# Gate and modulation vectors transposed on TensorE and written to DRAM as 512-byte rows

## Chip, core and metric

The kernel runs on one core of a Trainium2 chip. The time is device time in microseconds (us) from start to end of the program. The engines are PE (TensorE; PEld is its weight load), DVE (VectorE), ACT (ScalarE), POOL (GpSimd) and SP (SyncE, which issues all DMAs that matter here; its queue is called SPq in the rows). SP works its DMAs off in order: one that waits for data holds those behind it.

## The reference, cut to what matters

Two trunk layers run on 256 latent tokens `x` and 256 context tokens, of width 1024. Layer 0 is a gMLP mixer and a dense SwiGLU; layer 1 is an RG-LRU mixer and a mixture of 8 experts. Each sub-layer has this frame:

```python
sh1, sc1, gt1, sh2, sc2, gt2 = split(silu(c) @ ada_w[i] + ada_b[i], 6)   # 1024 numbers each
h = rmsnorm(x, norm_g[i, 0]) * (1 + sc1) + sh1
x = x + gt1 * rmsnorm(mixer(h), norm_g[i, 1])
x = x + gt2 * rmsnorm(channel_mixer(rmsnorm(x, norm_g[i, 2]) * (1 + sc2) + sh2), norm_g[i, 3])
```

The context has its own six vectors from `c_ctx`. The gate `gt * norm_g` is one number per channel, the same for all tokens. The last sub-layer also needs scale and shift as rows, since its tokens lie on partitions.

## The kernel before, in words

**Stages.** The weights come as 69 blocks of 1 MB (`in_wA`) in the order of `_weight_order` (L53): gMLP (`v`, `u`, `w`), dense feed-forward (`fg`, `fu`, `fd`), RG-LRU (`lx`, `lg`, `lw`). Each block is split by ACT (L249, the high part `wh`) and DVE (L250, the remainder `wl`), and used in three matmuls per product (L504 to L506 and L520 to L522). After about 880 us the experts run on raw weights (`in_wM`, 336 blocks).

**Stream.** Class `Stream` (L192) issues the loads on SP into a ring of raw buffers, four of them in the stretch at issue. A buffer is loaded again when DVE has read it. Three pairs of `wh`/`wl` buffers hold split weights ahead of PE.

**The adaLN matrix.** From block 3 on, 40 blocks of 1 MB of `in_adaT` stand among the weight blocks in the same ring. DVE multiplies each with the broadcast SiLU vector and sums along the row (L388, tile `dj`), so the six vectors of a layer come out as columns: channel `k*128 + p` lies on partition `p`, column `k`, of a `[128, 8]` tile.

**Columns to rows.** `gate_col` (L434) makes a gate column with two DVE operations (L436, L437). `rows_out` (L440) writes each column to DRAM by one DMA, L443:

```python
nc.sync.dma_start(d[i].rearrange("(k p) -> p k", p=P), c)
```

On the DRAM side neighbours of one partition lie 128 elements apart, so 1024 numbers go out one by one. `rows_in` (L446) reads the row back, broadcast to 128 partitions. There are four places, eight columns in all:

- `grd` (L723): layer 0's first gate for context and latent, written after unit W2 in the code, read into `gr`, used in `finish` (L678) of the first `turn` (L669).
- `gr2d` (L843): layer 0's second gate, after the fourth down-projection unit (`fd` 3), read into `gr2` at once, used in the second `turn`.
- `mrd` (L1005): layer 1's first gate and the coefficients `mca`, `mcb`, read into `mrow` at L1038.
- `god` (L1006): layer 1's second gate, read into `grow` at L1466, for the last step.

**Order.** Every engine runs its own instruction list in order. The lists are not the order of the code: when the program is built, a planner gives each engine the next instruction that is ready by its cost figures, the earlier in the code first. So operations with early data can stand far ahead of their place in the code. PSUM has eight banks, handed out by `bank()` (L275).

Of the kernel before, what the change touches and what calls it, by code (L numbers as in the profile page):

```python
# [9 lines left out]
F32 = mybir.dt.float32  # L10
# [7 lines left out]
P = 128  # L18
D = 1024
# [249 lines left out]
def block_kernel(ctx, tc, xin, pos, cst, rows, wsT, adaS, adaT, wA, lruG, wr, wM, out):  # L269
    nc = tc.nc  # L270
    ACT, DVE, PE = nc.scalar, nc.vector, nc.tensor
# [3 lines left out]
    bank = lambda: psx[0].tile([P, 512], F32, tag="ps", name="ps")  # L275
# [6 lines left out]
    pre = PRE.enter_context(pool("pre"))  # L282

    k = pre.tile([P, NCOL], F32, name="k")
# [6 lines left out]
    ident = perm.tile([P, P], F32, name="ident")  # L291
# [27 lines left out]
    PAIRS = (0, 1)  # L319
    VEC = (1, 0)  # L320
# [110 lines left out]
            do(b0, b1)  # L431
        return a, b, do

    def gate_col(l, s, gi, vv):  # L434
        g = pre.tile([P, 8], F32, name=f"cg{l}{s}{vv}")
        DVE.tensor_add(g, adaC[l, s][:, :, vv], K(f"adab{l}")[:, s * 8:s * 8 + 8])  # L436
        DVE.tensor_mul(g, g, ng(l, gi))  # L437
        return g

    def rows_out(cols, name):  # L440
        d = tc.dram_tile([len(cols), D], F32, name=name)
        for i, c in enumerate(cols):
            nc.sync.dma_start(d[i].rearrange("(k p) -> p k", p=P), c)  # L443
        return d

    def rows_in(dst, d):  # L446
        nc.sync.dma_start(dst, d.partition_broadcast(P))
# [68 lines left out]
    def ws(o, w, cb, c0, c1):  # L516
        wh, wl = w
        for kk in range(8):
            r = slice(kk * 256 + cb * P, kk * 256 + (cb + 1) * P)
            PE.matmul(o, wh[:, r], hThi[:, kk, c0:c1], start=(kk == 0), stop=False)  # L520
            PE.matmul(o, wh[:, r], hTlo[:, kk, c0:c1], start=False, stop=False)  # L521
            PE.matmul(o, wl[:, r], hThi[:, kk, c0:c1], start=False, stop=(kk == 7))  # L522
# [72 lines left out]
    def v_norm():  # L595
        for t in range(4):
            DVE.bn_aggr(mv[:, t], bst[:, t])
        DVE.tensor_scalar(vv_, mv[:, :, 1], EPS, None, op0=ALU.add)
        rsqrt(vr, vv_, 4)
        for t in range(4):  # L600
            DVE.tensor_scalar(v[t], v[t], mv[:, t, 0:1], vr[:, t:t + 1], op0=ALU.subtract, op1=ALU.mult)
# [14 lines left out]
    def u_mm(i):  # L616
        w = st.get()
        bs = [bank(), bank()]
        for cb in range(2):
            ws(bs[cb], w, cb, 0, 512)  # L620
        return bs

    def unit_u(i, bs):
        gu = []
        for cb in range(2):
            g = tmp.tile([P, 512], F32, tag="gu", name="gu")
            ACT.activation(g, bs[cb], AF.Gelu_apprx_tanh)
            gu.append(g)
        for cb in range(2):
            c = 2 * i + cb  # L630
            m = bank()
            for n in range(4):
                PE.matmul(m[:, n * P:(n + 1) * P], v[n][:, c * P:(c + 1) * P], wst[:, i], start=True, stop=True)
            t = tmp.tile([P, 512], F32, tag="t512", name="t")
            DVE.scalar_tensor_tensor(t.rearrange("p (n t) -> p n t", n=4), m.rearrange("p (n t) -> p n t", n=4), gv[:, c:c + 1],
                                     bsr[:, i][:, None, :].to_broadcast([P, 4, P]), op0=ALU.mult, op1=ALU.add)
            DVE.tensor_mul(t, t, gu[cb])
            split(c, t)

    def w_half(q, hf, first):  # L640
        w = st.get()
        banks = [bank() for _ in range(4)]
        ts(banks, pH, pL, w, range(4), 4, True, True, kb0=4 * q)
        for t in range(4):
            ys = ysum[:, t, hf * 512:(hf + 1) * 512]
            if first:
                ACT.copy(ys, banks[t])
            else:
                DVE.tensor_add(ys, ys, banks[t])

    def unit_w(q, first):
        for hf in range(2):
            w_half(q, hf, first)
        for c in range(4 * q, 4 * q + 4):
            prods.pop(c)
# [13 lines left out]
    def turn(last_w, last_mm, first_w, first_mm, X, gr, cf, before_t, nw):  # L669
# [42 lines left out]
                first_mm(n, ws_[n], p)  # L712
        return mid

    bu = [u_mm(0), u_mm(1)]
    v_norm()
    for s in ("U0", "U1", "U2", "W0", "U3", "U4", "W1", "U5", "U6", "W2"):
        if s[0] == "U":
            i = int(s[1])
            unit_u(i, bu[i] if i < len(bu) else u_mm(i))  # L720
        else:
            unit_w(int(s[1]), s == "W0")
    grd = rows_out([gate_col(0, 2, 1, VEC[p]) for p in PAIRS], "grd")  # L723
    w7 = st.get()
    p7 = [[php.tile([P, 512], F32R, tag=n, name=n) for n in ("ph", "pl")] for _ in range(2)]

# [72 lines left out]
    def unit_f(j, evac):  # L799
        w = st.get()  # L800
        banks = []
        for cb in range(2):
            b = bank()
            ws(b, w, cb, 0, 512)
            banks.append(b)
        evac(j, banks)
# [28 lines left out]
    for it in ORDER[24 + 4:]:  # L835
        if it[0] == "fg":
            unit_f(it[1], fg_evac)
        elif it[0] == "fu":
            unit_f(it[1], fu_evac)
        elif it[0] == "fd" and it[2] == 0 and it[1] < 4:  # L840
            unit_w(it[1], it[1] == 0)
            if it[1] == 3:
                gr2d = rows_out([gate_col(0, 5, 3, VEC[p]) for p in PAIRS], "gr2d")  # L843
                gr2 = xcp.tile([P, 2, D], F32, tag="gr", name="gr2")
                rows_in(gr2, gr2d)
    cfl = [coef(1, 0, 1, 0, VEC[p]) for p in PAIRS]
# [32 lines left out]
    def conv(c, b, seg):  # L879
        if c not in xq:  # L880
            xq[c] = php.tile([P, 2, 256], F32, tag="ph" if c < 6 else "pl", name="xq")
        for s in seg:
            src = b[:, 256 * s:256 * s + 256]
            o = xq[c][:, s]
            DVE.tensor_scalar(o, src, cw[:, 16 + c:17 + c], cbias[:, c:c + 1], op0=ALU.mult, op1=ALU.add)
            for kk, off in ((0, -2), (1, -1), (3, 1)):
                lo, hi = max(0, -off), 256 - max(0, off)
                DVE.scalar_tensor_tensor(o[:, lo:hi], src[:, lo + off:hi + off], cw[:, kk * 8 + c:kk * 8 + c + 1], o[:, lo:hi], op0=ALU.mult, op1=ALU.add)
# [21 lines left out]
    def queued():  # L910
        return tc.issue_after(act_last[0].ins) if act_last[0] is not None else nullcontext()
# [25 lines left out]
    def gates_exp(j):  # L937
        R_, I_, T_ = RIT.pop(j)
        hs[j] = php.tile([P, 2, 256], F32, tag="pl", name="hs")
        last = None  # L940
        with queued():
            act_last[0] = ACT.preload_act_table_set("natural_log_exp_and_others")
        with queued():
            for cb in range(2):
                t, i, a = T_[cb], I_[cb], R_[cb]
                ACT.activation(t, t, AF.Ln, bias=tiny[:, 0:1])
                ACT.activation(t, t, AF.Exp, scale=0.5)
                for d in range(2):
                    col = slice(d * 8 + 2 * j + cb, d * 8 + 2 * j + cb + 1)
                    last = ACT.activation(a[:, d], a[:, d], AF.Exp, scale=nspl[:, col])  # L950
                DVE.scalar_tensor_tensor(t, a, 1.0, t, op0=ALU.add, op1=ALU.mult)
                DVE.tensor_tensor(out=i, in0=i, in1=t, op=ALU.mult)
                DVE.tensor_tensor_scan(t[:, 0], a[:, 0], i[:, 0], 0.0, ALU.mult, ALU.add)
                rv = lambda z, s: z[:, 1, 256 * s:256 * s + 256][:, ::-1]
                DVE.tensor_tensor_scan(rv(t, 0), rv(a, 0), rv(i, 0), 0.0, ALU.mult, ALU.add)
                DVE.tensor_tensor_scan(rv(t, 1), rv(a, 1), rv(i, 1), t[:, 1, 0:1], ALU.mult, ALU.add)
                DVE.tensor_add(hs[j][:, cb], t[:, 0, 256:512], t[:, 1, 256:512])
        act_last[0] = last

    def unit_x(j):  # L960
        w = st.get()
        for cb in range(2):
            b = bank()
            ws(b, w, cb, 0, 512)
            conv(2 * j + cb, b, (0, 1))
# [3 lines left out]
    def unit_g(j):  # L969
        w = st.get()  # L970
        b = bank()
        for cb in range(2):
            ws(b[:, cb * 256:(cb + 1) * 256], w, cb, 256, 512)
        gbs[j] = b
# [27 lines left out]
        DVE.tensor_tensor(out=f(yl), in0=h2, in1=f(yh).bitcast(F32), op=ALU.subtract)  # L1002

    mca, mcb, _ = coef(1, 3, 4, 2, 0)
    mrd = rows_out([gate_col(1, 2, 1, 0), mca, mcb], "mrd")  # L1005
    god = rows_out([gate_col(1, 5, 3, 0)], "god")  # L1006
    unit_x(3)
    gates_exp(1)
    unit_g(0)
    gates_sig(2)  # L1010
# [24 lines left out]
    R = ExitStack()  # L1035
    rp = R.enter_context(pool("rp", 1, "right"))
    mrow = hTp.tile([P, 4, D], F32, tag="hThi", name="mrow")
    rows_in(mrow[:, 0:3], mrd)  # L1038
    iot = rp.tile([P, 256], I32, name="iot")
    nc.gpsimd.iota(iot, pattern=[[1, 256]], base=1, channel_multiplier=0)  # L1040
    slot = mp.tile([P, 256], F32, name="slot")
# [421 lines left out]
                DVE.tensor_scalar(Ys[E.s][:, 512:1024], E.base.y[1], E.base.ps, None, op0=ALU.mult)  # L1463
    ACT.preload_act_table_set("sqrt_and_others")
    grow = mw.tile([P, D], F32, name="grow")
    rows_in(grow[:, None, :], god)  # L1466
    mj = ta_.bitcast(BF16)
    ssf = small.tile([P, 4], F32, tag="ss", name="ssf")
    rsf = small.tile([P, 4], F32, tag="rstd", name="rsf")
# [32 lines left out]
```

## Time and profile before

| What | us |
|---|---|
| Median of 3 runs | 1881.88 (1878.27 to 1882.68) |
| The profiled execution | 1881.16 |
| Its span, first to last instruction | 1879.2 |
| PE busy | 1685.1 (90%) |
| DVE busy | 832.9 (44%) |
| ACT busy | 572.3 (30%) |
| Mean granted PE clock | 0.961 of full speed |

Busy time is a mean over stages with different limits. The windows view gives it by stretch: busy time of each engine, instructions in brackets, the granted clock, the busy share of the 16 DMA engines and what they moved. In the timeline each row is an instruction; a square bracket gives how long its engine stood idle before it and what released it.

### The profile page before, as it was taken

The page shows a single profiled execution, that of the slowest core. Times are in us where ns is not written, and L with a number is a line of the kernel's source. Part 1 is how long each engine was busy: PE and PEld are TensorE (multiplying, and loading weights), DVE is VectorE, ACT ScalarE, POOL GpSimd, SP SyncE. Part 2 cuts the span into 40 slices and gives each one's busy share as a digit, 9 for nine tenths or more (in the row PEclk, how much of TensorE's full clock was granted, in tenths as well). Part 3 has the DMA queues.
Part 4 walks back from the last instruction along what each step waited for, and adds up shares of the span by engine and source line. Part 5 has one row for each costly group of instructions (what it writes and reads, how often), then busy time and mean ns, then how long its engine had stood idle before and what let it go on. Part 6 is the DMA issues. An engine that isn't in the chain of part 4 may idle for free. (4 is left out here: it accounts for less than half of the span.)

```text
span 1879.2 us, 21723 instructions
## 1 busy us (share of the span) xinstructions
PE 1685.1 (90%) x8189; PEld 1034.8 (55%) x8189; DVE 832.9 (44%) x1340; ACT 572.3 (30%) x837; POOL 19.4 (1%) x22
## 2 busy tenths in 40 slices
PE   5999999998997999997678789988998999889987
PEld 2888888987885788775324233333433344333332
DVE  3768746566964538896322222224111112222233
ACT  5523224732221227893221112211111112122221
POOL 0000001000000000001000000000000000000000
PEclk8999999999998899999789899999998999999999
DMA  8554424247775622246697769896899899979990
GB/s 355 210 171 157 157 90 158 105 174 175 275 189 182 187 97 79 68 174 270 275 416 308 303 266 379 364 397 262 363 417 419 367 395 360 403 312 388 401 401 23
DMA packets 78629, 492.97 MB, mean 262 GB/s; under 512 B 16240, under 2 KB 16368, under 8 KB 20080
## 3 DMA queue, kind: packets, MB, share of 16 engines
q1 hardware_dynamic: 78448, 490.45, 68.1%
q8 instruction: 127, 2.08, 0.4%
q14 instruction: 54, 0.44, 0.1%
HBM read 489.34 MB, written 1.08 MB: 261 GB/s over the span
## 5 line engine op out<-in xcount | busy, mean ns | idle before, releaser
L1263 PE MATMUL ps<-raw,x 128*64 128x512 f32 (+2 forms) x1792 | 441.7, 613 | 28.3 <-PEq L1351 11.9
L1263 PEld LDWEIGHTS ps<-raw,x 128*64 128x64 f32 (+2 forms) x1792 | 162.8, 143 | 261.5 <-issue 244.7
L1290 PE MATMUL ps<-raw,hx 128*32 128x512 f32 (+2 forms) x1120 | 259.2, 626 | 18.2 <-ACT hx L1282 15.1
L520 PE MATMUL ps<-hThi,wh 128*128 128x512 f32 (+1 forms) x736 | 254.3, 347 | 3.0 <-ACT hThi L373 3.0
L521 PE MATMUL ps<-hTlo,wh 128*128 128x512 f32 (+1 forms) x736 | 253.1, 344 | 1.3 <-DVE hTlo L374 1.3
L522 PE MATMUL ps<-hThi,wl 128*128 128x512 f32 (+1 forms) x736 | 253.5, 345 | 0.0
L1270 DVE TENSOR_TENSOR ta__6625<-ps,ta__6625 64x512 f32<-64x512 f32 x112 | 76.5, 683 | 350.3 <-ACT ta__6625 L1269 350.3
L388 DVE SCALAR_TENSOR_TENSOR dj<-raw,srow 128x1024 bf16<-128x1024 f32 x128 | 156.3, 1221 | 93.3 <-DMA raw<-in_adaT_dram 89.9
L249 ACT CAST wh<-raw 128x2048 fp32r<-128x2048 f32 x69 | 131.4, 1908 | 203.7 <-PE ps L506 95.5
L250 DVE TENSOR_TENSOR wl<-raw,wh 128x2048 fp32r<-128x2048 f32 x69 | 158.8, 2304 | 58.7 <-ACT wh L249 58.2
L1290 PEld LDWEIGHTS ps<-raw,hx 128*32 128x32 f32 (+2 forms) x1120 | 92.3, 138 | 161.9 <-issue 123.1
L1269 ACT COPY ta__6625<-ps 64x512 f32<-64x512 f32 x112 | 65.2, 582 | 302.4 <-PE ps L1263 292.3
L520 PEld LDWEIGHTS ps<-hThi,wh 128*128 128x128 f32 x736 | 138.7, 189 | 21.8 <-ACT hThi L373 3.7
L521 PEld LDWEIGHTS ps<-hTlo,wh 128*128 128x128 f32 x736 | 138.8, 189 | 20.5 <-DVE hTlo L374 1.7
L522 PEld LDWEIGHTS ps<-hThi,wl 128*128 128x128 f32 x736 | 138.9, 189 | 17.5 <-issue 0.5
L504 PE MATMUL ps<-wh,ph 128*128 128x512 f32 x304 | 122.7, 404 | 17.3 <-ACT ph L609 17.3
L506 PE MATMUL ps<-wh,pl 128*128 128x512 f32 x304 | 121.4, 400 | 6.7 <-DVE pl L610 6.3
L1296 DVE TENSOR_TENSOR hx<-hx,ps 128x512 f32<-128x512 f32 x14 | 9.6, 688 | 252.3 <-PE ps L1263 177.8
L505 PE MATMUL ps<-wl,ph 128*128 128x512 f32 x304 | 120.2, 395 | 0.0
L1282 ACT COPY hx<-ps 128x128 f32<-128x128 f32 (+2 forms) x70 | 25.3, 361 | 225.0 <-PE ps L1281 223.3
L1263 PE MATMUL ps<-raw,xu 128*32 128x512 f32 x448 | 69.5, 633 | 21.6 <-DVE accy L1318 11.4
L504 PEld LDWEIGHTS ps<-wh,ph 128*128 128x128 f32 x304 | 58.3, 192 | 30.2 <-ACT ph L609 18.2
(318 smaller groups left out, 1669.2 us busy)
## 6 DMA issues: line engine op xcount, KB each, us to landing
raw<-in_wM_dram SPq DMA_DIRECT2D x336, 1024.0 KB, 13.7
raw<-in_wA_dram SPq DMA_DIRECT2D x69, 1024.0 KB, 4.9
raw<-in_adaT_dram SPq DMA_DIRECT2D x40, 1024.0 KB, 5.4
va<-in_adaS_dram SPq DMA_DIRECT2D x4, 1024.0 KB, 10.6
ysum<-in_xin_dram SPq DMA_DIRECT2D x4, 512.0 KB, 5.3
vb<-in_adaS_dram SPq DMA_DIRECT2D x2, 1024.0 KB, 10.8
srow<-in_adaS_dram SPq DMA_DIRECT2D x2, 1024.0 KB, 12.2
lw<-in_lruG_dram SPq DMA_DIRECT2D x8, 256.0 KB, 3.1
```

The source lines that it names most:

```text
L249: self.nc.scalar.copy(wh, raw)
L250: self.nc.vector.tensor_tensor(out=wl, in0=raw, in1=wh.bitcast(F32), op=ALU.subtract)
L388: DVE.scalar_tensor_tensor(j, raw[:, kk * D:(kk + 1) * D], 1.0, srow[:, vv], op0=ALU.mult, op1=ALU.mult, accum_out=adaC[l, bb // 8][:, bb ...
L504: PE.matmul(o, lh, rh, start=start, stop=False)
L505: PE.matmul(o, lh, rl, start=False, stop=False)
L506: PE.matmul(o, ll, rh, start=False, stop=stop)
L520: PE.matmul(o, wh[:, r], hThi[:, kk, c0:c1], start=(kk == 0), stop=False)
L521: PE.matmul(o, wh[:, r], hTlo[:, kk, c0:c1], start=False, stop=False)
L522: PE.matmul(o, wl[:, r], hThi[:, kk, c0:c1], start=False, stop=(kk == 7))
L1263: PE.matmul(o[m * g:m * g + m], x[:, kb, 0:m], raws[kb // 4][1][:, (kb % 4) * 512:(kb % 4 + 1) * 512], start=(r == 0), stop=(r == 8 // n - ...
L1270: DVE.tensor_tensor(out=ta_[0:64], in0=o[0:64], in1=ta_[0:64], op=ALU.add)
L1290: PE.matmul(yb_[hf][m * g:m * g + m], U.th[:, kk * m:(kk + 1) * m], rd[hf][1][:, kk * 512:(kk + 1) * 512], start=(first and r == 0), stop= ...
```

## The change

The columns of one place are gathered in one tile (`gcol`, `mcol`), so `gate_col` writes into a slice of it. `rows_out` transposes that tile on PE against the identity into a PSUM bank, ACT copies the `[8n, 128]` result to SBUF, and one DMA writes it as `8n` rows of 512 bytes. `mrd` and `god` become one tensor of four rows, for which DVE copies `mca` and `mcb` into `mcol`. In the code the gate columns move ahead of W2 and of `fd` 3, and the write of `mrd` moves behind `unit_x(3)`.

```diff
-    def gate_col(l, s, gi, vv):
-        g = pre.tile([P, 8], F32, name=f"cg{l}{s}{vv}")
+    def gate_col(g, l, s, gi, vv):
         DVE.tensor_add(g, adaC[l, s][:, :, vv], K(f"adab{l}")[:, s * 8:s * 8 + 8])
         DVE.tensor_mul(g, g, ng(l, gi))
-        return g
-
-    def rows_out(cols, name):
-        d = tc.dram_tile([len(cols), D], F32, name=name)
-        for i, c in enumerate(cols):
-            nc.sync.dma_start(d[i].rearrange("(k p) -> p k", p=P), c)
+
+    def rows_out(cols, n, name):
+        d = tc.dram_tile([n, D], F32, name=name)
+        m = 8 * n
+        b = bank()
+        PE.transpose(b[0:m, 0:P], cols.rearrange("p n k -> p (n k)"), ident)
+        r = pre.tile([32, P], F32, tag="rowT", name="rowT")
+        ACT.copy(r[0:m], b[0:m, 0:P])
+        nc.sync.dma_start(d.rearrange("n (k p) -> (n k) p", p=P), r[0:m])
         return d
...
+    gcol = pre.tile([P, 4, 8], F32, name="gcol")
...
+            if s == "W2":
+                for p in PAIRS:
+                    gate_col(gcol[:, p], 0, 2, 1, VEC[p])
             unit_w(int(s[1]), s == "W0")
-    grd = rows_out([gate_col(0, 2, 1, VEC[p]) for p in PAIRS], "grd")
+    grd = rows_out(gcol[:, 0:2], 2, "grd")
...
+            if it[1] == 3:
+                for p in PAIRS:
+                    gate_col(gcol[:, 2 + p], 0, 5, 3, VEC[p])
             unit_w(it[1], it[1] == 0)
             if it[1] == 3:
-                gr2d = rows_out([gate_col(0, 5, 3, VEC[p]) for p in PAIRS], "gr2d")
+                gr2d = rows_out(gcol[:, 2:4], 2, "gr2d")
                 gr2 = xcp.tile([P, 2, D], F32, tag="gr", name="gr2")
                 rows_in(gr2, gr2d)
...
     mca, mcb, _ = coef(1, 3, 4, 2, 0)
-    mrd = rows_out([gate_col(1, 2, 1, 0), mca, mcb], "mrd")
-    god = rows_out([gate_col(1, 5, 3, 0)], "god")
+    mcol = pre.tile([P, 4, 8], F32, name="mcol")
+    gate_col(mcol[:, 0], 1, 2, 1, 0)
+    gate_col(mcol[:, 3], 1, 5, 3, 0)
+    for n, c in ((1, mca), (2, mcb)):
+        DVE.tensor_copy(mcol[:, n], c)
     unit_x(3)
+    mrd = rows_out(mcol, 4, "mrd")
...
-    rows_in(mrow[:, 0:3], mrd)
+    rows_in(mrow[:, 0:3], mrd[0:3])
...
-    rows_in(grow[:, None, :], god)
+    rows_in(grow[:, None, :], mrd[3:4])
```

## Rows read from the trace of the kernel before

**Rows 1.** Windows: window, its length, PE, PEld, DVE, ACT, POOL busy, clock, DMA share, GB/s.
```profile
400.00:450.00 50.00, 50.00 (x220) 41.01 (x219) 37.27 (x55) 13.23 (x14) 0.00 (x0) 1.00 0.59 132
450.00:500.00 50.00, 43.72 (x183) 35.27 (x182) 36.91 (x52) 9.15 (x7) 0.00 (x0) 0.93 0.64 232
...
600.00:650.00 50.00, 35.15 (x138) 27.58 (x139) 29.70 (x37) 10.27 (x9) 0.00 (x0) 0.80 0.65 189
...
800.00:850.00 50.00, 46.26 (x244) 35.36 (x242) 46.63 (x49) 46.56 (x58) 0.34 (x1) 0.97 0.52 191
```

**Rows 2.** Timeline of PE around its long stops: start, us, engine, line, operation.
```profile
464.71 0.80 PE L506 MATMUL ps<-wh,pl 128*128 128x512 f32 x1 [6.28 <-DVE pl L610]
...
468.19 0.40 PE L505 MATMUL ps<-wl,ph 128*128 128x512 f32 x1
...
610.36 0.79 PE L504 MATMUL ps<-wh,ph 128*128 128x512 f32 x1 [12.77 <-ACT ph L609]
...
616.74 0.80 PE L504 MATMUL ps<-wh,ph 128*128 128x512 f32 x1 [4.50 <-ACT ph L609]
...
621.77 0.39 PE L506 MATMUL ps<-wh,pl 128*128 128x512 f32 x1
```

**Rows 3.** Timeline of DVE: its long waits for blocks of the adaLN matrix.
```profile
462.81 1.22 DVE L388 SCALAR_TENSOR_TENSOR dj<-raw,srow 128x1024 bf16<-128x1024 f32 x1 [16.86 <-DMA raw<-in_adaT_dram]
...
543.00 1.23 DVE L388 SCALAR_TENSOR_TENSOR dj<-raw,srow 128x1024 bf16<-128x1024 f32 x1 [10.42 <-DMA raw<-in_adaT_dram]
...
603.21 1.23 DVE L388 SCALAR_TENSOR_TENSOR dj<-raw,srow 128x1024 bf16<-128x1024 f32 x1 [12.43 <-DMA raw<-in_adaT_dram]
```

**Rows 4.** Timeline of SP's issues around the writes of L443.
```profile
432.57 0.43 SPq L443 DMA_DIRECT2D gr2d<-cg  x1
455.02 0.33 SPq L447 DMA_DIRECT2D gr<-gr2d  x1
...
520.71 0.41 SPq L443 DMA_DIRECT2D mrd<-cg  x1
...
587.72 3.17 SPq L222 DMA_DIRECT2D raw<-in_adaT_dram  x2
590.98 0.39 SPq L443 DMA_DIRECT2D mrd<-ca  x1
```

**Rows 5.** DMA issues of the whole span: count, KB each, median us to landing.
```profile
raw<-in_adaT_dram SPq DMA_DIRECT2D x40, 1024.0 KB, 5.4
...
out_dram<-xl SPq DMA_DIRECT2D x4, 256.0 KB, 2.1
```

**Rows 6.** DMA issues between 590 and 590.9 us, in the same columns.
```profile
raw<-in_adaT_dram SPq DMA_DIRECT2D x1, 1024.0 KB, 12.6
```

**Rows 7.** By line: duration min/median/max, first and last start, forms.
```profile
L1054 PE MATMUL ps<-wrt,cb x16: 170/256/256, 844.8 to 846.3; 128*128 128x8 f32 x16
...
L427 DVE TENSOR_TENSOR cb<-ada,k x9: 156/163/167, 22.4 to 551.2; 128x8 f32<-128x8 f32 x5, 128x4 f32<-128x4 f32 x4
...
L436 DVE TENSOR_TENSOR cg<-ada,k x6: 158/162/166, 98.5 to 630.3; 128x8 f32<-128x8 f32 x6
```

**Rows 8.** Groups of instructions by line: count, busy us, mean ns.
```profile
L1282 ACT COPY hx<-ps 128x128 f32<-128x128 f32 (+2 forms) x70 | 25.3, 361 | 225.0 <-PE ps L1281 223.3 <-ACTq L1351 0.5 <-ACT ps L1272 0.4
...
L367 PE MATMUL ps<-ident,ysum 128*128 128x128 f32 x96 | 13.2, 294 | 0.0
```

**Rows 9.** Timelines of PE, ACT, SP and DVE at the first use of a row.
```profile
289.35 0.28 PE L520 MATMUL ps<-hThi,wh 128*128 128x256 f32 x1
...
289.55 1.91 ACT L249 CAST wh<-raw 128x2048 fp32r<-128x2048 f32 x1 [9.08 <-PE ps L506]
...
296.93 0.33 SPq L447 DMA_DIRECT2D gr<-grd  x1
...
291.50 2.29 DVE L250 TENSOR_TENSOR wl<-raw,wh 128x2048 fp32r<-128x2048 f32 x1 [1.26 <-ACT wh L249]
```

**Rows 10.** Timeline of SP where the last rows are read back.
```profile
829.83 0.33 SPq L447 DMA_DIRECT2D mrow<-mrd  x1
```

## The prediction, made before the change was run

> **What bounds the kernel now.** I read the windows first. In a good stretch of the trunk PE has no gap: from 400 to 450 us it is busy 50.00 of 50 us at full clock, beside DVE at 37.27 [rows 1]. So whatever PE loses in the trunk is lost by the whole program, since the expert stage starts when the trunk ends. Two later windows show losses: 43.72 and 35.15 us of 50, at a clock of 0.93 and 0.80 [rows 1].
>
> The timeline of PE says where: it stops for 6.28 us before 464.71, for 12.77 before 610.36 and for 4.50 before 616.74, together 23.55 us, and each time the row names ACT's or DVE's split of an activation (L609, L610) as the releaser [rows 2]. The splits themselves are short. The timeline of DVE shows why they are late: DVE, in order, stands before L388 and waits for a block of the adaLN matrix, 16.86 us until 462.81 and 12.43 us until 603.21; a third of 10.42 us, and another like it in between, cost PE nothing [rows 3].
>
> The timeline of SP shows what is in front of each. At 432.57 SP writes a gate column; at 455.02 it issues the read of that row, which had to wait for the landing: 455.02 - 432.57 = 22.4 us in which SP issued no load [rows 4]. Three columns of `mrd` go out between 520.71 and 590.98, and a long wait of DVE ends 12 to 22 us behind each of them; the first is 543.00 - 520.71 = 22.3, the last 603.21 - 590.98 = 12.2 [rows 3, 4]. A block of the adaLN matrix lands after 5.4 us in the median [rows 5]; the one issued at about 590.6, just ahead of the column of 590.98, took 12.6 us [rows 6]. So a column of 4 KB holds up a load of 1 MB by about 7 us.
>
> **The change part by part.**
>
> *Columns become rows of 512 bytes.* Eight DMAs of 1024 single numbers become three DMAs of 16, 16 and 32 rows. The landing of such a write is not in the trace. Below it is bounded by the write of whole rows to DRAM, `out_dram`, 2.1 us for 256 KB [rows 5]; above by what the column took, 22.4 us [rows 4]. I take 2.1, since whole rows are what it is. Then SP's hold before the read of `gr2d` shrinks by some 20 us, the four waits of DVE go, and PE's three stops with them.
>
> What that gives PE, with the slow clock behind each stop. At full clock a matmul takes 50.00 / 220 = 0.227 us [rows 1]. First place: 6.28 us of stop, and then 9 matmuls from 464.71 to the start of the ninth at 468.19, 3.48 us where 8 x 0.227 = 1.8 would do, 1.7 more. Loss 7.9 us. Second place: 12.77 us of stop, and then 15 matmuls with the stop of 4.50 among them, 621.77 - 610.36 = 11.41 us where 14 x 0.227 = 3.2 would do. Loss 21.0 us [rows 2]. Sum 28.9 us, of which 23.55 are stops and 5.4 matmuls at the lower of the two clock levels. Lower bound of the gain: nothing, if the blocks are late for another reason (a rival). What is late next: DVE has 37.27 us of work in 50 [rows 1] and the later adaLN blocks need one vector instead of two, so DVE stays ahead of PE; I leave nothing standing.
>
> *The transposes.* Three on PE. The nearest row is L367, 0.294 us each [rows 8]: 0.9 us on PE, all on the path, as PE has no gap there. Bounds 0 (hidden in a gap) and 3 x 0.6 with a wait on the weight load. Where they stand in PE's list: a small PE operation whose column was ready at 551.2 (L427, last start) ran only at 844.8, its place in the code [rows 7]. DVE and SP work is pulled far forward (gate columns from 98.5 us on [rows 7]), PE work is not. So I expect them behind W2, behind `fd` 3 and behind `unit_x(3)`, with their columns long ready, and PE waits for none. Queued behind them on PE are the matmuls of U7, of `fu` 8 and of the RG-LRU gates. If one did wait, each us would count in full.
>
> *The ACT copies.* Three, at most 0.361 us (L1282, [rows 8]). Two stand where ACT has time (13.23 us of 50, [rows 1]); the third lies in the RG-LRU stage, where ACT is near its limit (46.56 of 50 us, [rows 1]), and I count 0.36. If it lands behind a batch of gate functions it delays only `mrd`, which is not read before 829.83 [rows 10]. Queued behind each copy on ACT is a weight split (1.91 us, [rows 9]) with PE some blocks away.
>
> *New wait on SP.* SP now waits for PE and ACT before it can write a row, and loads queue behind it. `grd`: at 289.35 PE is in U7, so W2 is done; ACT may first do a split of 1.91 us, so the write goes at 292 and lands at 294; SP reads it back at 296.93 anyway [rows 9], so nothing changes. `gr2d`: written behind `fd` 3, read 60 us before its use; SP holds for 2.1 us. `mrd`: its four columns leave 520 to 631 us and go out in one write behind `unit_x(3)`, past SP's loads for `lx`; behind it on SP are the gate weights of the RG-LRU stage, and its read comes some 50 us later [rows 10]. The cover is measured: 22.4 us without a load, with a slow landing behind it, cost PE 6.28 us of stop [rows 2, 4], so about 15 us are free. I cost it at 0.
>
> *Gate columns and copies on DVE.* The twelve operations stay; two copies come, 0.16 us each by L436 [rows 7], in time that DVE has. 0.
>
> *Sum.* 1881.16 (the profiled execution, 0.7 us under the median of the runs) - 28.9 + 0.9 + 0.4 = 1853.6; against the median 1854.
>
> The Trainium skill says on its page "DMA: Bandwidth & Descriptors" (Queues, rings and completion order) that a DMA's semaphore write lands only after every earlier write of that DMA engine. By that rule a column can hold only loads issued after it, and the block of 590.6 was issued before the column of 590.98. The trace disagrees as far as it goes: that block took 12.6 us [rows 6] with only the column queued behind it. The rule's case is the first rival below.
>
> **The rivals.**
>
> *A: the long stop has another cause.* The block that DVE waited for until 603.21 was issued ahead of the column [rows 3, 4]; if a column holds only what comes behind it, that block was late for a reason of its own, and the 21.0 us stay. For: its place in the queue. Against: 12.6 us of landing against a median of 5.4, only beside a column [rows 5, 6]. Time: 1881.16 - 7.9 + 1.3 = 1874.6. This is the case of the Trainium skill's rule above.
>
> *B: the columns are not the cause at all.* The adaLN blocks crowd the four buffers, and PE stops where DVE is behind. For: all stops lie in the stretch with those blocks. Against: DVE is idle for 12 and 17 us before them [rows 3], so it was not behind in work. Time: 1881.16 + 1.3 = 1882.5.
>
> *C: SP stands behind PE (slower).* At the three places SP's list may have the write ahead of loads that PE needs next. SP then waits for PE's transpose, buffers run dry, and PE idles once per place: landing 5.4 [rows 5], ACT's split 1.91 and DVE's 2.29 [rows 9], and slow clock 1.7 [rows 2], 11.3 us; at `grd` and `gr2d` the landing of the write, 2.1, comes on top, and at `gr2d` the read of 1 MB, another 5.4. Sum 11.3 x 3 + 2.1 x 2 + 5.4 = 43.5 us. Time 1853.6 + 43.5 = 1897. It turns slower when these idle times pass 28 us in all. For: the hold of 22.4 us shows that SP's list can stand at a wait while loads are due. Against: the 15 us of cover, and that SP's list keeps loads ahead of PE by all its buffers.
>
> **How the numbers follow.** Forecast 0.73, A 0.12, B 0.07, C 0.08. A gain of 7 us is over 0.3% (5.6 us, about what a measurement can tell from none), so A counts as faster, B as same, and C as slower but for a mild form: faster 0.86, same 0.07, slower 0.07. The forecast's own range runs from 1849, if the columns' absence also removes the 3.7 us that PE lacks between 800 and 850 us (46.26 of 50, [rows 1]), to 1863, if a third of the 28.9 us stays. To hold eight in ten the upper end must take in A: 1848 to 1876.
>
> **What would show it.** Right: no read of `gr2d` 22 us behind its write; landings of about 2 us for `grd`, `gr2d`, `mrd`; no wait of DVE over 6 us for `in_adaT`; PE at 50 of 50 with clock 1.00 in the windows from 450 to 650; the expert stage starting 28 us earlier and as long as before. Wrong: a stop of PE at the transposes' releasers, SP waiting for ACT at L443's successor with PE idle behind it, or the stop near 600 us still there (A).

## The result, and the profile after

The changed kernel takes 1852.13 us (median of 4 runs, 1844.61 to 1853.17), the kernel before 1880.08 beside it: ratio 0.984, 95% interval 0.981 to 0.987. The forecast was 1854.0; the gain of 28.0 us was forecast as 27.9. In the experiments, further runs gave 1852.21 for the changed kernel and about 1873 for the kernel before, so the gain there was 21 us. Why the kernel before was 7 us quicker in those runs is open, and it is compared only with runs beside it.

The profiled execution of the changed kernel took 1844.61 us (span 1842.8), the shortest of its four. First its windows, in the columns of [rows 1]:

```profile
400.00:450.00 50.00, 50.00 (x220) 41.10 (x219) 43.87 (x64) 14.65 (x16) 0.00 (x0) 1.00 0.55 198
450.00:500.00 50.00, 50.00 (x220) 41.12 (x219) 45.98 (x71) 12.29 (x10) 0.00 (x0) 1.00 0.74 265
...
600.00:650.00 50.00, 50.00 (x221) 40.97 (x220) 17.11 (x16) 11.76 (x12) 0.00 (x0) 1.00 0.35 127
...
800.00:850.00 50.00, 42.75 (x236) 36.13 (x234) 40.88 (x121) 24.15 (x42) 9.31 (x10) 0.90 0.71 279
```

The two windows that lost 6.3 and 14.9 us are full, at clock 1.00. The same window from 600 now holds a later part of the program: DVE has 17.11 us of work in it, where it had 29.70. The window from 800 cannot be compared with its row of before, as the program is 33 us further on there.

DVE's waits for a block of the adaLN matrix, where [rows 3] had 16.86, 10.42 and 12.43 us; these are the three longest that stand between 425 and 620 us:

```profile
518.17 1.22 DVE L388 SCALAR_TENSOR_TENSOR dj<-raw,srow 128x1024 bf16<-128x1024 f32 x1 [3.91 <-DMA raw<-in_adaT_dram]
...
561.80 1.23 DVE L388 SCALAR_TENSOR_TENSOR dj<-raw,srow 128x1024 bf16<-128x1024 f32 x1 [4.39 <-DMA raw<-in_adaT_dram]
...
584.52 1.23 DVE L388 SCALAR_TENSOR_TENSOR dj<-raw,srow 128x1024 bf16<-128x1024 f32 x1 [5.63 <-DMA raw<-in_adaT_dram]
```

The new chain at its second place, in order of time: PE's transpose, ACT's copy, SP's write and SP's read (start, us, engine, line).

```profile
606.37 0.27 PE L442 MATMUL ps<-ident,gcol 128*16 128x128 f32 x1
606.40 0.48 PE L522 MATMUL ps<-hThi,wh 128*128 128x512 f32 x1
606.57 1.91 ACT L249 CAST wh<-raw 128x2048 fp32r<-128x2048 f32 x1 [8.97 <-PE ps L508]
606.72 0.40 PE L523 MATMUL ps<-hTlo,wh 128*128 128x512 f32 x1
...
608.39 0.25 ACT L444 COPY rowT<-ps 16x128 f32<-16x128 f32 x1
608.66 0.33 SPq L445 DMA_DIRECT2D gr2d<-rowT  x1
610.84 0.34 SPq L222 DMA_DIRECT2D raw<-in_wA_dram  x1
611.22 0.42 SPq L449 DMA_DIRECT2D gr<-gr2d  x1
```

Between write and read of `gr2d` there are 2.6 us, where [rows 4] had 22.4, and a load of weights goes out in between. The transpose has no wait in its row and the next matmul starts 0.03 us behind it. The other two look the same, at 287.89 and 760.16. The copy stands 2 us behind the transpose because a split of weights (1.91 us) is ahead of it on ACT.

The DMA issues of the whole span (count, KB each, median us to landing), against [rows 5]:

```profile
raw<-in_adaT_dram SPq DMA_DIRECT2D x40, 1024.0 KB, 4.9
...
grd<-rowT SPq DMA_DIRECT2D x1, 8.0 KB, 1.4
...
gr2d<-rowT SPq DMA_DIRECT2D x1, 8.0 KB, 1.3
mrd<-rowT SPq DMA_DIRECT2D x1, 16.0 KB, 1.4
```

And SP's waits for the new copies (total, count, longest):

```profile
SPq L445 <- ACT rowT L444: 22.2, 3, 8.4
```

So SP does stand before the three writes, as rival C said, for 22.2 us in all. PE has no wait in its timeline behind any of the three.

Where the time came from, by two marks: the last of ACT's copies to `ysum` (L647 before, L649 after) starts at 412.0 before and 409.2 after, DVE's last addition to it (L649, L651) at 639.4 and 606.6. So 32.8 - 2.8 = 30.0 of the 36.6 us between the two profiled executions were gained in the stretch with the adaLN blocks. Of the rest 2.8 us were gained ahead of it and 3.8 behind it. The experts' routing (L1150, L1163) starts at 873.2 before and 839.1 after, 34.1 us earlier where the forecast had 28; the last 2.5 us lie behind that.

### The profile page after: what moved, and what is told of

It reads as the page before. It is cut to its first block, busy times and chain, and to the rows that moved or that the text cites. A ratio compares the mean times of both kernels' runs of the same rounds, so it can differ in the third digit from the quotient of the medians.

```text
span 1842.8 us, 21730 instructions
## 1 busy us (share of the span) xinstructions
PE 1667.9 (91%) x8192; PEld 1026.5 (56%) x8192; DVE 835.5 (45%) x1342; ACT 573.8 (31%) x840; POOL 19.4 (1%) x22
## 5 line engine op out<-in xcount | busy, mean ns | idle before, releaser
L523 PEld LDWEIGHTS ps<-hTlo,wh 128*128 128x128 f32 x736 | 138.1, 188 | 20.8 <-DVE hTlo L374 2.0
L1286 DVE TENSOR_TENSOR ta__6629<-ps,ta__6629 32x512 f32<-32x512 f32 x70 | 47.5, 678 | 38.0 <-ACT ps L1285 34.2
```

## The experiments

Two theories stood at the outset. *Form*: a column of single numbers is slow and holds the 1 MB loads in the DMA; DVE gets its adaLN blocks late, and PE its activations. *Place*: transposing made the writes late, behind the adaLN loads, and it is this move that gained. Later a third question came up, what in a column is slow. "Last sum" is the start of the last addition to `ysum` in the profile, the mark at which the stretch ends.

| kernel | median us (runs) | ratio to the kernel before, 95% | last sum |
|---|---|---|---|
| changed kernel, again | 1852.21 (6) | 0.9878 [0.9851, 0.9905] | 608.8 |
| `gr2d` by columns | 1855.96 (6) | 0.9907 [0.9880, 0.9933] | 612.0 |
| `mrd`, `god` by columns | 1858.18 (6) | 0.9918 [0.9892, 0.9945] | 617.5 |
| both | 1872.77 (12) | 0.9983 [0.9968, 0.9997] | 629.0 |
| columns at the new places | 1868.52 (12) | 0.9979 [0.9962, 0.9995] | 620.5 |
| rows near the old places | 1850.56 (5) | 0.9863 [0.9842, 0.9885] | 608.3 |
| dummies, 1024 x 4 B, close | 1867.98 (10) | 0.9962 [0.9943, 0.9980] | 626.0 |
| dummies, 128 x 32 B | 1851.90 (4) | 0.9868 [0.9844, 0.9891] | 607.8 |
| dummies, 1024 x 64 B | 1853.07 (6) | 0.9893 [0.9865, 0.9921] | 608.5 |
| dummies, 4 B, ACT's queue | 1860.28 (7) | 0.9930 [0.9904, 0.9956] | 619.6 |
| dummies, 1024 x 4 B, spread | 1852.04 (6) | 0.9872 [0.9851, 0.9893] | 608.4 |
| dummies, 1024 x 16 B | 1851.91 (6) | 0.9870 [0.9846, 0.9893] | 608.3 |

The first row is the control. Its expectation:

> The changed kernel once more, as the yardstick for the other runs on this chip. Both theories: 1845 to 1853 us, 28 to 33 us under the kernel before.

Its time lies in the expected range. The gap does not: 20.8 us in place of 28 to 33, since the kernel before took 1872.96 beside it.

**One place undone at a time.** In both, a helper writes the columns as the kernel before did:

```
+    def rows_out_e(cols, name):
+        d = tc.dram_tile([len(cols), D], F32, name=name)
+        for i, c in enumerate(cols):
+            nc.sync.dma_start(d[i].rearrange("(k p) -> p k", p=P), c)
+        return d
...
-                gr2d = rows_out(gcol[:, 2:4], 2, "gr2d")
+                gr2d = rows_out_e([gcol[:, 2 + p] for p in PAIRS], "gr2d")
```

> The changed kernel with gr2d alone written column by column again, one number per packet. Theory (each place's single-number writes cost what PE lost there): the first stop of PE is back, 7.9 us, so about 1860 us; SP stands some 22 us before the read of gr2d, and DVE waits about 17 us for an adaLN block behind it. Rival (the stops were one chain, and the buffers cover a single place): no more than 2 us over the changed kernel, 1854 us.

It lost 3.8 us, between the 7.9 of the theory and the 2 of the rival. The timeline of SP, DVE and PE has the chain of the forecast's first place:

```profile
431.71 0.43 SPq L451 DMA_DIRECT2D gr2d<-gcol  x1
450.31 0.33 SPq L455 DMA_DIRECT2D gr<-gr2d  x1
...
458.90 1.23 DVE L388 SCALAR_TENSOR_TENSOR dj<-raw,srow 128x1024 bf16<-128x1024 f32 x1 [13.83 <-DMA raw<-in_adaT_dram]
460.79 0.50 PE L514 MATMUL ps<-wh,pl 128*128 128x512 f32 x1 [3.22 <-DVE pl L618]
```

SP is held for 18.6 us, DVE for 13.83, and PE stops for 3.22 us, half of the 6.28 in [rows 2]. Near 600 us PE does not stop. The mechanism is there, at half its size.

Then the other place (the two reads, changed to match, are left out):

```
-    for n, c in ((1, mca), (2, mcb)):
-        DVE.tensor_copy(mcol[:, n], c)
+    mrd = rows_out_e([mcol[:, 0], mca, mcb], "mrd")
+    god = rows_out_e([mcol[:, 3]], "god")
     unit_x(3)
-    mrd = rows_out(mcol, 4, "mrd")
```

> The changed kernel with mrd and god alone written column by column again, at once when each column is ready. Theory: the stops near 600 us are back, 21.0 us, so about 1873 us, with three waits of DVE of 10 to 13 us for adaLN blocks. Rival (the buffers cover a single place; the stops near 600 us were the debt of gr2d's hold at 432 us): 1854 to 1860 us, with the waits of DVE there but PE stopped under 6 us.

It lost 6.0 us, not 21; the rival (1854 to 1860 us, PE stopped under 6 us) had this. The window where it lost:

```profile
550.00:600.00 50.00, 45.68 (x188) 36.61 (x187) 28.65 (x39) 11.70 (x12) 0.00 (x0) 0.94 0.62 228
```

DVE waits 9.05, 10.89 and 7.39 us for blocks, and PE stops once, for 4.3 us. The losses of one place alone, 3.8 and 6.0, make 9.8 of the 20.8 us that the whole change gains there. The intervals of these two ratios overlap that of the control, so the two sizes are rough; that either place costs something is read from PE's stops. So either the rest is something else, or the two are not independent. That was asked next.

**Both places undone.** The two edits above in one kernel, so that it differs from the kernel before by `grd` alone (and by where the gate columns stand in the code).

> The changed kernel with both gr2d (read back at once, as in the kernel before) and mrd and god (written ahead of unit_x(3)) column by column again, one number per packet; grd stays as rows. Beside the kernel before this differs by grd alone. Undone one at a time they cost 3.8 and 6.0 us. Theory of a common debt: gr2d's hold uses up the lead that VectorE and the loads have on TensorE, and the columns of mrd, 70 us later, find no lead; so together they cost about twice the sum of the two, 17 to 23 us, and the time is within 5 us of the kernel before (ratio 0.997 to 1.003), with a TensorE stop of 8 us or more between 590 and 620 us. Rival (two separate losses): they add up to 9.8 us, ratio 0.994 or less to the kernel before, and no TensorE stop above 5 us.

It is back at the kernel before (1872.77 against 1873.33), 20.6 us over the changed kernel. PE's waits (total, count, longest) and its windows:

```profile
PE ps L512 <- ACT ph L617: 12.7, 2, 7.4
...
PE ps L514 <- DVE pl L618: 2.8, 1, 2.8
```

```profile
450.00:500.00 50.00, 47.16 (x200) 38.34 (x200) 41.19 (x62) 8.90 (x7) 0.00 (x0) 0.97 0.74 259
...
550.00:600.00 50.00, 44.58 (x190) 35.46 (x188) 28.33 (x39) 8.27 (x8) 0.00 (x0) 0.97 0.63 168
600.00:650.00 50.00, 42.72 (x180) 34.72 (x181) 25.11 (x29) 10.88 (x10) 0.00 (x0) 0.89 0.64 197
```

The first place costs 2.8 us of stop, about as it does alone (3.22); the second costs 12.7 where it costs 4.3 alone. The last sum moves by 20.2 us, where one place at a time moves it by 3.1 and 8.7. So the columns of `gr2d` take mostly lead (the time by which loads and DVE run ahead of PE), and PE shows the loss only when the columns of `mrd` come. One miss: the longest single stop is 7.4 us, not 8 or more; the loss came in two stops. And `grd`, whose columns are the only ones left out, is worth little: 0.6 us between the medians, at most 6 by the interval.

**Form or place.** The columns are copied by DVE behind the unit that the transposes stand behind, and written from there one number per packet:

```
+    def rows_late(cols, n, name):
+        r = pre.tile([P, 4, 8], F32, tag="rowL", name="rowL")
+        with tc.issue_after(last_dve[0].ins):
+            DVE.tensor_copy(r[:, 0:n], cols)
+        return rows_out_e([r[:, i] for i in range(n)], name)
...
-    grd = rows_out(gcol[:, 0:2], 2, "grd")
+    grd = rows_late(gcol[:, 0:2], 2, "grd")
...
```

> The changed kernel without transposes: the columns are copied by DVE behind W2, fd 3 and unit_x(3) and written from there one number per packet, so the writes stand where the changed kernel has them, outside the adaLN stretch. Theory (the form of the write costs): 22 us holds of SP now stand before the reads of grd and gr2d, and the four columns of mrd block the loads of the RG-LRU stage for some 4 x 12 us; about 1890 us (1870 to 1905). Rival (the place and the number of DMAs were what cost, not the form): 1852 us, as the changed kernel.

It lost 16.3 us (the time is just below the expected 1870 to 1905), though in no window from 350 to 700 us did PE miss a tenth of a us. The loss is at the other two places: DVE and PE near `grd`, and PE beside the write of `mrd`.

```profile
312.68 1.23 DVE L694 TENSOR_TENSOR ysum<-ysum,gr 128x1024 f32<-128x1024 f32 x1 [4.58 <-DMA gr<-grd]
322.82 1.22 PE L759 MATMUL ps<-wst,vb 128*128 128x128 f32 x4 [4.44 <-DVE t L760]
...
807.00 8.87 PE L949 MATMUL ps<-xq,lw 128*128 128x512 f32 x16 [6.89 <-DMA lw<-in_lruG_dram]
```

A column is dear at these places too, where a transfer beside it is about to be needed. Gate weights of the RG-LRU (256 KB) issued beside the columns of `mrd` landed after 21.0 us in the median. A part of the 16.3 us has another cause: PE's steps are about 1% longer all through this kernel, also without a gap. The window from 400 to 450, here and in the repeat of the changed kernel:

```profile
400.00:450.00 50.00, 50.00 (x218) 40.70 (x217) 37.35 (x54) 15.59 (x18) 0.00 (x0) 1.00 0.53 193
```

```profile
400.00:450.00 50.00, 50.00 (x221) 41.09 (x220) 41.65 (x60) 15.66 (x16) 0.00 (x0) 1.00 0.54 193
```

Why 218 matmuls fit where 221 did, no row shows; up to the last sum it is some 3 us. The reverse test leaves rows, but moves their writes towards the places of the kernel before:

```
+            if it[1] == 2:
+                gate_col(mcol[:, 0], 1, 2, 1, 0)
+                mrd0 = rows_out(mcol[:, 0:1], 1, "mrd0")
             if it[1] == 3:
...
+                mrd1 = rows_out(mcol[:, 1:3], 2, "mrd1")
+            if it[1] == 1:
                 for p in PAIRS:
                     gate_col(gcol[:, 2 + p], 0, 5, 3, VEC[p])
...
                 gr2d = rows_out(gcol[:, 2:4], 2, "gr2d")
```

> The changed kernel, still with rows of 512 bytes, but transposed and written near the places of the kernel before, inside the stretch of the adaLN loads: gr2d behind fd(1), mrd's first vector behind fd(2), its second and third behind fd(3), god's behind fu(8); five writes of rows in place of three. Theory (the form of the write is what counts, not its place): 1852 to 1857, ratio to the kernel before 0.986 to 0.992, the written rows land in less than 3 us and SP is held less than 5 us at a read of the rows. Rival (the place beside the loads is what cost the time, and writing behind the loads is what gained): it loses 4 to 21 us against the changed kernel, ratio 0.990 to 1.0, with stops of TensorE at ph and pl between 440 and 620 us.

1850.56 us, no loss: PE is at 50.00 of 50 in each window from 400 to 650, and `gr2d` landed after 2.3 us. But only two of the writes stand among the adaLN loads, as SP's timeline shows:

```profile
478.65 0.33 SPq L445 DMA_DIRECT2D gr2d<-rowT  x1
...
544.53 0.34 SPq L445 DMA_DIRECT2D mrd<-rowT  x1
...
580.72 0.33 SPq L222 DMA_DIRECT2D raw<-in_adaT_dram  x1
```

The last line is the last adaLN load; the other two writes go out at 610.41 and 621.80. So two writes of rows among the loads cost nothing, and columns outside the stretch still cost time. The place theory has fallen on the second count; on the first it has only the two rows against it.

**Is it SP's hold or the DMA?** The forecast put the first place down to SP, which issues no load until the column has landed. Here the changed kernel also writes each column to a dummy that nobody reads, so SP never waits for one:

```
+    def dummy(c, name):
+        d = tc.dram_tile([1, D], F32, name=name)
+        nc.sync.dma_start(d[0].rearrange("(k p) -> p k", p=P), c)
...
                     gate_col(gcol[:, 2 + p], 0, 5, 3, VEC[p])
+                    dummy(gcol[:, 2 + p], f"xb{p}")
```

> The changed kernel, with each of the eight vectors also written, one number per packet, to a dummy tensor as soon as VectorE has made it (two ahead of W2's units, two ahead of fd(3), four ahead of unit_x(3)); nobody reads the dummies, so SP is never held for them. 8192 packets of 4 bytes are added. Theory (the packets themselves hold the loads in the DMA queues): loads of adaT beside them land 10 us or later, VectorE waits for raw 7 us or more there, and the time rises by 4 to 16 us over the changed kernel (ratio to the kernel before 0.990 to 0.998). Rival (only SP, held at the read of the rows until the slow write has landed, costs time): within 2 us of the changed kernel, ratio 0.987 to 0.989.

It lost 15.8 us, the upper end of the range, with no wait of SP for the landing of a column. A load of weights that SP issued at 430.74, between the two columns of the first place, was slow (the issues from 430.6 to 430.9):

```profile
raw<-in_wA_dram SPq DMA_DIRECT2D x1, 1024.0 KB, 19.0
```

So were the adaLN loads behind it, as the theory had them (the issues from 429 to 447, median):

```profile
raw<-in_adaT_dram SPq DMA_DIRECT2D x2, 1024.0 KB, 16.8
```

Near 600 us PE stops again; at the first place it does not, as its window and DVE's longest wait there show:

```profile
450.00:500.00 50.00, 50.00 (x221) 41.07 (x220) 44.95 (x71) 12.70 (x12) 0.00 (x0) 1.00 0.73 252
```

```profile
454.78 1.23 DVE L388 SCALAR_TENSOR_TENSOR dj<-raw,srow 128x1024 bf16<-128x1024 f32 x1 [10.29 <-DMA raw<-in_adaT_dram]
...
597.57 0.80 PE L510 MATMUL ps<-wh,ph 128*128 128x512 f32 x1 [10.14 <-ACT ph L615]
...
603.47 0.80 PE L510 MATMUL ps<-wh,ph 128*128 128x512 f32 x1 [4.01 <-ACT ph L615]
```

The last sum is at 626.0 us, against 629.0 where SP is held as well. So slow transfers without any hold make 17 of the 20 us that columns cost in this stretch (15.8 of 20.6 by the medians), and SP's hold adds the rest. What a hold without slow transfers costs was not tried.

**What in a column is slow.** The same dummies in five variants, at the same places; each changes how the numbers are cut into packets, where they go, or the queue. First 128 packets of 32 bytes for a column:

```
-        nc.sync.dma_start(d[0].rearrange("(k p) -> p k", p=P), c)
+        nc.sync.dma_start(d[0].rearrange("(p k) -> p k", p=P), c)
```

> As the dummy writes of single numbers, at the same places and with the same bytes, but each column is written as 128 packets of 32 bytes (the eight numbers of a partition side by side) in place of 1024 packets of 4 bytes. Theory (what holds the loads is the number of packets, eight times fewer here): a dummy lands in 2 to 4 us, VectorE's waits for raw stay below 7 us, and the time is within 2 us of the changed kernel (ratio to the kernel before 0.986 to 0.990). Rival (small packets as such, or one more write among the loads, cost the time): the same loss as with the single numbers, 4 us or more.

No loss (1851.90), though some dummies landed later than the 2 to 4 us expected, those of `xc` after 4.6 to 6.5. That could be the number of packets or their size. So 1024 packets with 64 bytes each, every number copied 16 times first:

```
+        d = tc.dram_tile([D, 16], F32, name=name)
...
+        DVE.tensor_copy(w, c[:, :, None].to_broadcast([P, 8, 16]))
+        nc.sync.dma_start(d.rearrange("(k p) j -> p k j", p=P), w)
```

> As the dummy writes of single numbers (eight columns, never read, same places), but each of the 1024 packets of a column carries 64 bytes in place of 4: VectorE first copies each number 16 times (eight more copies, estimated at 0.3 us each). Theory (the number of packets makes a write slow and holds the loads, whatever they carry): the same loss as with the packets of 4 bytes, the dummies land in 10 to 18 us, VectorE waits for raw 7 us or more beside them, ratio to the kernel before 0.990 to 1.000. Rival (packets below some size, here 4 bytes, are slow each for their size): landings below 6 us and a time within 2 us of the changed kernel, ratio 0.986 to 0.990.

1853.07, no loss, with as many packets as the costly kernel. The dummies landed after 5.0 to 7.2 us, a little over the 6 of the rival. The lines on DMA packets of the two pages, that of the 4-byte dummies first:

```profile
DMA packets 78741, 493.01 MB, mean 265 GB/s; under 512 B 16288, under 2 KB 16480, under 8 KB 20192
```

```profile
DMA packets 78741, 493.50 MB, mean 267 GB/s; under 512 B 16288, under 2 KB 16480, under 8 KB 20192
```

Both have 16288 packets under 512 bytes. My theory that the number of packets decides has fallen. Next, the 4-byte packets from ACT's DMA queue (`nc.scalar.dma_start` in place of `nc.sync.dma_start`):

> As the dummy writes of single numbers by 4 bytes, at the same places in the program, but issued from ScalarE's DMA queue in place of SP's, so that they don't stand ahead of the loads in the queue that issues the loads. Theory A (the packets occupy the shared DMA engines, whatever queue they come from): loads of adaT beside them land 10 us or later, and the time rises as with SP's queue, ratio to the kernel before 0.990 to 1.000. Theory B (a queue works its writes off in order, and only loads of the same queue are held): loads land in 6 us or less, VectorE's waits for raw stay below 7 us, the time is within 3 us of the changed kernel, ratio 0.986 to 0.990.

8.1 us lost: within A's range, but half of what the same packets cost in SP's queue. A's mechanism is there: the load that SP issued at 431.40, with no column in its own queue, took this long:

```profile
raw<-in_wA_dram SPq DMA_DIRECT2D x1, 1024.0 KB, 13.8
```

and DVE waited up to 10.99 us. So the other queue softens the slowing and does not lift it. The Trainium skill says in "DMA: Bandwidth & Descriptors" (Issuing engines are not separate DMA queues) that SP's and ACT's queues share the same 16 engines; the 13.8 us agree.

Last, size against neighbours: 4-byte packets, of which each has 64 bytes of HBM to itself, and packets of 16 bytes side by side.

```
-        d = tc.dram_tile([1, D], F32, name=name)
-        nc.sync.dma_start(d[0].rearrange("(k p) -> p k", p=P), c)
+        d = tc.dram_tile([D, 16], F32, name=name)
+        nc.sync.dma_start(d[:, 0].rearrange("(k p) -> p k", p=P), c)
```

> As the dummy writes of single numbers (eight columns of 1024 packets of 4 bytes, never read, same places in SP's queue), but in HBM each number has 64 bytes to itself: it is written to the first 4 bytes of a line of 64, so no two packets touch the same 64 bytes. The same number of packets with 64 bytes each cost nothing. Theory L (several packets that write parts of the same 64 bytes hold one another up): landings below 7 us, VectorE's waits for raw below 7 us, the time within 3 us of the changed kernel, ratio to the kernel before 0.985 to 0.991. Theory S (a write of 4 bytes is slow by itself, wherever it goes): landings of 10 us or more and the loss of the dummies of 4 bytes, ratio 0.993 to 1.000.

No loss: 1852.04, with the same bytes in as many 4-byte packets, from the same tiles, in the same queue. Theory L had this. The dummies of both kernels, spread first and then close (DMA issues, median us to landing):

```profile
xa<-gcol SPq DMA_DIRECT2D x2, 4.0 KB, 4.0
xb<-gcol SPq DMA_DIRECT2D x2, 4.0 KB, 6.0
...
xc<-cb SPq DMA_DIRECT2D x1, 4.0 KB, 5.6
```

```profile
xa<-gcol SPq DMA_DIRECT2D x2, 4.0 KB, 11.7
xb<-gcol SPq DMA_DIRECT2D x2, 4.0 KB, 16.1
...
xc<-cb SPq DMA_DIRECT2D x1, 4.0 KB, 13.6
```

The load at the place of the 19.0 us (issued at 431.28 here) took:

```profile
raw<-in_wA_dram SPq DMA_DIRECT2D x1, 1024.0 KB, 6.5
```

So a write of 4 bytes is not slow by itself; it is when its neighbours in HBM are written beside it. The Trainium skill gives 512 bytes as the least transfer for full rate and says that below it the engine reads, modifies and writes ("DMA: Bandwidth & Descriptors", Specifications). All five shapes of the dummies lie under 512 bytes; four of them cost nothing here, so in this case the measurement decides for something narrower.

The packets of 16 bytes are those of 64 with 4 copies of each number in place of 16 (against that kernel):

```
-        d = tc.dram_tile([D, 16], F32, name=name)
+        d = tc.dram_tile([D, 4], F32, name=name)
...
```

> As the dummy writes of 64-byte packets, but 1024 packets of 16 bytes for each of the eight columns, side by side in HBM, four to each 64 bytes (VectorE copies each number 4 times first). Theory L (packets that write parts of the same 64 bytes hold one another up): landings between those of 4 bytes (12 to 16 us) and those of 64 bytes (5 to 7 us), some 7 to 12 us, and a loss between none and the 16 us of the dummies of 4 bytes. Theory S (a write of less than some size is slow, wherever it goes): if that size is above 16 bytes the full loss and landings of 10 us or more, if below none and landings below 7 us. With the spread packets of 4 bytes this tells whether size or sharing counts.

1851.91, no loss; the dummies landed after 5.6, 8.2 and 6.6 us. Theory L had expected some loss. Sharing 64 bytes among four packets costs nothing in the time, so sharing as such is not enough. Between four packets of 16 bytes and sixteen of 4 lies the point where it becomes slow. Which piece of HBM must be shared, and whether the order of the packets matters, was not tried. Nor was this rival: spread, or 16 bytes each, the 1024 packets also cover 64 or 16 KB of HBM in place of 4, so it may be the small range that counts and not the shared 64 bytes.

## Why the prediction was right, and where it was not

*The total.* The mechanism, slow column, late block, idle DVE, PE's stop, is shown by undoing it and by bringing it back with dummies. That the gain agrees to 0.1 us is luck. The same two kernels gave 20.8 us in the experiments, and undoing both places cost 20.6 there. The 28.9 us were read from one execution of the kernel before, of 1881.16 us, where later ones took 1865.6 to 1882.7; no trace of a quicker one was kept. And the expert stage, from L1163 to the end, took 1003.7 us in one profile of the changed kernel and 1010.6 in the other.

*The landing.* Taken as 2.1 us, measured 1.3 to 1.4. SP's hold at `gr2d` went from 22.4 to 2.6 us. Right.

*The gain in the stretch.* Forecast 28.9, measured 30.0 between the two profiles. Right for the profile it was read from. But the step "first place 7.9, second place 21.0, sum 28.9" failed as a split. Alone the two cost 3.8 and 6.0 us in the experiments, together 20.6. The stops were counted where PE showed them; the lead that the first place used up was paid at the second. A sum over stops is right for undoing all of them and wrong for undoing one.

*The cause of the first place.* The forecast gave it to SP, "in which SP issued no load". At the place itself that is right in part: with dummies, so without a hold, DVE still waits 10.29 us, against 13.83 where `gr2d` alone goes by columns, but PE does not stop. For the whole stretch the hold is the smaller part: without it the last sum is late by 17.1 of 20.2 us, since loads beside and behind the columns land late and the lead is missing at the second place.

*Transposes.* Forecast 3 x 0.294 us on PE at their place in the code, with no wait. The place was right and the rows read 0.27. But the steps of PE from 606.40 to 606.72 and around it make one transpose worth about 0.12 us (0.03 + 0.32 - 0.23), so 0.9 was too much by some 0.5 us.

*ACT's copies* took 0.25 us where 0.36 was the bound, each behind a split as drawn; *DVE's two copies* show nowhere. *SP's new wait* was costed at 0 by a cover of about 15 us: it came to 22.2 us in three parts, the longest 8.4, each inside the cover, and PE stops behind none.

*Rivals.* A (the load ahead of the column is late for a reason of its own) has fallen: its time was 1874.6 against 1852 measured, the long stops near 600 are gone, and dummies bring them back. The dummies of 4 bytes also have a block issued just ahead of a column (the load's issue at about 580.5, the column's at 580.95; DMA issues from 580.2 to 580.9):

```profile
raw<-in_adaT_dram SPq DMA_DIRECT2D x1, 1024.0 KB, 9.9
```

It took twice the median of 5.0, less than the 12.6 of [rows 6] and than the 16.8 of loads behind columns: a load just ahead of a column is late too, by less. The prediction took its cited rule for more than it says: the rule tells what a landing waits for, not that a load already out cannot be slowed. B (columns not the cause) has fallen with A. C had its wait, but not its price. The columns' absence did not also remove the 3.7 us between 800 and 850 us: from the last addition to `ysum` to the first matmul of L1054 (L1067 after) the kernel before takes 844.8 - 639.4 = 205.4 us and the changed one 811.8 - 606.6 = 205.2.

## What to carry to other kernels

Before writing a vector that lies across partitions to DRAM number by number, bring it into rows: here three transposes and three copies of a quarter microsecond each together bought back 21 to 28 us. The price of these transfers was not in their own rows but in the loads beside them, so look at the landing of the large loads issued around a small one. And where one late transfer eats the lead that the next one needs, undo both before judging either.

## What was not expected of the hardware

- A 1 MB load issued between two columns, each 1024 packets of 4 bytes written close together, landed after 19.0 us; with as many packets spread by 64 bytes after 6.5. As many of 64 bytes cost the program nothing (1853.07 us).
- The slowing crosses queues: with the columns in ACT's queue a load in SP's took 13.8 us.
- Of PE, 0.27 us of transpose between two matmuls moves the next one by only 0.03 us and those behind it by another 0.1.
